# Row norm factors between two blocks: applied to the rows before the transpose, or where the products leave PSUM

## Chip, core and metric

One NeuronCore of one Trainium2 chip. The metric is the device time of one execution in microseconds (us), median of several runs. The engines are named as in the profile: PE (TensorE matmul), PEld (its weight load), DVE (VectorE), ACT (ScalarE), POOL (GpSimd), SP (SyncE, which here only issues DMAs).

## The reference

Two transformer-like blocks follow each other on 512 tokens of width 1024. The first ends with an RMS norm (gain `g_final`), the second begins with another (gain `norm_mix_g_2`) and a projection by `w_in_2`, whose output is cut into a GLU for a 31-tap causal convolution, queries, keys, values, forget logits and two gates:

```python
def rmsnorm(x, g):
    y = xf * lax.rsqrt(jnp.mean(xf * xf, axis=-1, keepdims=True) + EPS)
    return (y * g.astype(jnp.float32)).astype(x.dtype)

x = first_block(...)          # returns rmsnorm(x, g_final)
h = rmsnorm_2(x, norm_mix_g[l])
proj = h @ w_in[l]
u_glu, q, k, v, f_logit, gate_c, gate_a = jnp.split(proj, cuts, axis=-1)
```

A token's norm factor is one number for its row, so it commutes with the product by `w_in_2`. With s the mean square of x, and p that of x times `g_final`, the two norms together are x times `g_final` times `norm_mix_g_2` times one factor per token.

## The kernel before

All matrices are float32. In the second block a product is made of three: each operand is split into a rounded high part H and a low part L (`wsplit`, `split`), and `mm3` (line 86) issues H by H, H by L and L by H into one PSUM tile. A split is an ACT copy (line 131) and a subtraction (line 132) that POOL does, or DVE where said so.

`phase_b` is the first block's expert layer, eight pairs of experts. Its last pair ends with `last_down` (products line 1182, one PSUM tile for each half e of the width) and `scatter` (lines 1202 to 1216): the tile is scaled (y), split (yH on ACT, yL on DVE), multiplied by a 0/1 matrix P that puts rows back to their tokens, one product for each group t of 128 tokens, and added into `xres` by DVE (line 1216). Ahead of it, 16 small products and 4 ACT copies (lines 1234 and 1235) spread both gains over 128 partitions into `gg`.

`phase_c` begins with the norm. For each token group t and half e: `stage1` multiplies x by `g_final` (xg) and takes the sums of squares of x and xg on ACT (`sumsq`, line 1312); `stage2` makes the two factors r of the group (lines 1347 to 1351) and calls `put_T`, which multiplies xg by r and the second gain (hn, line 1323), transposes it on PE (line 1326) and splits it into `hx`, the moving operand of all projections. Then ACT writes xg times r back to `xres` (line 1363) and it goes to memory (`xrd`).

The projections follow: for each of 4 column tiles ct of the GLU a gate tile and a value tile (the first pair by `gemm_ws2`, in two halves of 256 tokens; the others by `ws_tile`, 24 products of 512 columns each), then the forget logits (fz), 8 tiles of queries and keys (`ev_qk`, line 1435), 4 of values by `gemm_ta`, and the gates. Their PSUM tiles come from a pool of four (tag "mm", `self.ps`); small products and transposes use another four (tag "at", `self.pa`). ACT empties every tile but the value tile of the GLU, which DVE multiplies by the gate (line 1381). Meanwhile DVE runs the convolution (lines 1400 to 1403): 31 taps for each ct, 124 instructions with 4 closing ones, in a row behind each other.

A scheduler sets the order of each engine's instructions at build time, with priorities (`tc.high_priority`) and hints (`tc.issue_after`); on the chip each engine takes its own instructions strictly in that order.

Of the kernel before, what the change touches and what calls it, by code (L numbers as in the profile page):

```python
# [8 lines left out]
F32 = mybir.dt.float32  # L9
# [8 lines left out]
EPS = 1e-6  # L18
# [27 lines left out]
XG = ((0, 0, 0, 0), (1, 1, 1, 1))  # L46
# [34 lines left out]
class Builder:  # L81
# [4 lines left out]
    def mm3(self, ps, l, r, first, last):  # L86
        mm = self.nc.tensor.matmul
        mm(ps, l[0], r[0], start=first, stop=False)  # L88
        mm(ps, l[0], r[1], start=False, stop=False)  # L89
        mm(ps, l[1], r[0], start=False, stop=last)  # L90
# [1039 lines left out]
    def phase_b(self, pb, right, G0):  # L1130
# [71 lines left out]
        def scatter(p, py):  # L1202

            P = xp.tile([128, 512], F32R, tag="PT", name="PT", bufs=1)
            V.tensor_scalar(P, self.iota, self.idxF[:, p:p + 1], None, op0=OP.is_equal)
            for e in range(2):
                y = xp.tile([128, 512], F32, tag="hid", name="y", bufs=3)
                V.scalar_tensor_tensor(y, py[e], self.valF[:, p:p + 1], ga2[:, e, :], op0=OP.mult, op1=OP.mult)  # L1208
                H, L = (xp.tile([128, 512], F32R, tag="yS", name=x, bufs=3) for x in ("yH", "yL"))
                AC.activation(out=H, in_=y, func=AF.Copy)  # L1210
                (nc.gpsimd if p < 7 else V).tensor_tensor(out=L, in0=y, in1=H, op=OP.subtract)  # L1211
                for t in range(4):
                    ps = self.pa()
                    self.mm2(ps, P[:, t * 128:(t + 1) * 128], (H, L), True, True)
                    c = slice(e * 512, (e + 1) * 512)
                    V.tensor_tensor((acc if p < 7 else xres)[:, t, c], (acc if p else xres)[:, t, c], ps, op=OP.add)
# [7 lines left out]
        for p in range(8):  # L1224
            hid = silu(pg)
            nxt = gather(p + 1) if p < 7 else None
            hT = hidden(hid, pair_mm(w_u, p, xT))
            if p == 7:
                gg = self.gg = self.rawp.tile([128, 2, 1024], F32, tag="raw", name="raw")
                for i in range(4):  # L1230
                    ps = self.pa()
                    for q in range(4):
                        r = 4 * i + q
                        nc.tensor.matmul(ps[:, q * 128:(q + 1) * 128], ident[0:16, r:r + 1].to_broadcast([16, 128]), rows2, start=True, stop=True)
                    AC.activation(out=gg[:, i // 2, (i % 2) * 512:(i % 2 + 1) * 512], in_=ps, func=AF.Copy)
# [40 lines left out]
    def phase_c(self, pc, right):  # L1276
# [34 lines left out]
        def sumsq(ss, src):  # L1311
            AC.activation(out=sm.tile([128, 512], F32, tag="nsq", name="nsq", bufs=2), in_=src, func=AF.Square, accum_out=ss)
# [18 lines left out]
        gf, g = self.gg[:, 0, :], self.gg[:, 1, :]  # L1331
        hx, ts = new_act()
        sss = [sm.tile([128, 2, 2], F32, tag="ss", name="ss", bufs=4) for _ in range(4)]
        xgs = [[tw(name="xg") for _ in range(2)] for _ in range(4)]
        r1s = {}

        def stage1(t, e):
            xs = xres[:, t, e * 512:(e + 1) * 512]
            (nc.gpsimd, V)[XG[e][t]].tensor_tensor(out=xgs[t][e], in0=xs, in1=gf[:, e * 512:(e + 1) * 512], op=OP.mult)
            sumsq(sss[t][:, 0, e:e + 1], xs)  # L1340
            sumsq(sss[t][:, 1, e:e + 1], xgs[t][e])

        def stage2(t):

            ss = sss[t]
            s, r = (sm.tile([128, 2], F32, tag=x, name=x, bufs=4) for x in ("s2", "r2"))
            V.tensor_tensor(s, ss[:, :, 0], ss[:, :, 1], op=OP.add)
            V.tensor_scalar(s, s, 1.0 / D, None, op0=OP.mult)
            V.tensor_scalar(s[:, 0:1], s[:, 0:1], EPS, None, op0=OP.add)
            V.scalar_tensor_tensor(s[:, 1:2], s[:, 0:1], EPS, s[:, 1:2], op0=OP.mult, op1=OP.add)  # L1350
            nc.gpsimd.tensor_tensor(out=r, in0=s, in1=self.mhalf.to_broadcast([128, 2]), op=OP.pow)
            r1s[t] = r[:, 0:1]
            put_T(ts, t, xgs[t], r[:, 1:2], g)
        for t in range(4):
            stage1(t, 0)
        stage1(0, 1)
        for t in range(4):
            if t < 3:
                stage1(t + 1, 1)
            stage2(t)  # L1360
        for t in range(4):
            for e in range(2):
                AC.activation(out=xres[:, t, e * 512:(e + 1) * 512], in_=xgs[t][e], func=AF.Copy, scale=r1s[t])

        xrd = self.drp.tile([512, 1024], F32, name="xrd")
        for t in range(4):
            nc.sync.dma_start(out=xrd[t * 128:(t + 1) * 128, :], in_=xres[:, t, :])
# [6 lines left out]
        def ev_gate(ct, ps):  # L1374
            glu[ct] = tw(name="glu")
            AC.activation(out=glu[ct], in_=ps, func=AF.Tanh, scale=0.5)

        def ev_a(ct, ps):
            u = sa.tile([128, 544], F32, tag="upad", name="upad", bufs=NST)
            nc.gpsimd.memset(u[:, 0:32], 0.0)  # L1380
            V.scalar_tensor_tensor(u[:, 32:544], glu[ct], 1.0, ps, op0=OP.add, op1=OP.mult)
            ups[ct] = u
        for c2 in (0, 256):
            rg, ra = self.cols_chunk(w, 512 + c2, 8, 256), self.cols_chunk(w, c2, 8, 256)
            for q in (0, 128):
                ct = (c2 + q) // 128
                pg, pa_ = (self.gemm_ws2([(rg, 0), (ra, 0)], hx) if ct == 0 else
                           (self.ws_tile(rg, q, hx, 8), self.ws_tile(ra, q, hx, 8)))
                ev_gate(ct, pg)
                ev_a(ct, pa_)  # L1390

# [26 lines left out]
        AC.activation(out=z, in_=ps[0:8], func=AF.Identity, bias=bf)  # L1418
# [21 lines left out]
        self.gemm_ta(w, 2048, hx, 8, 4, lambda t, ps: AC.activation(out=vt[t], in_=ps, func=AF.Copy))  # L1440
# [17 lines left out]
        on = sa.tile([128, 128], F32, tag="on128", name="on128", bufs=1)  # L1458
        V.memset(on, 1.0 / 512.0)
# [236 lines left out]
        V.memset(wrp, 0.0)  # L1696
        wr = wrp[:, :, 0:20]
        sel = sm.tile([128, 20], F32, tag="sel20", name="sel20", bufs=1)
        V.tensor_tensor(sel, ident[:, 0:20], ident[:, 32:52], op=OP.add)
        for q in (64, 96):  # L1700
            V.tensor_tensor(sel, sel, ident[:, q:q + 20], op=OP.add)
# [4 lines left out]
        V.tensor_tensor(wr, wr, gc.unsqueeze(2).to_broadcast([128, 8, 20]), op=OP.mult)  # L1706
# [461 lines left out]
```

## Time and profile before

| what | value |
|---|---|
| median of 3 runs | 1699.02 us (1697.12 to 1700.84) |
| the profiled execution, its own time | 1697.02 us |
| its span in the profile | 1695.0 us |
| granted TensorE clock, mean | 0.975 |
| PE busy | 92% of the span |
| DVE, ACT, POOL busy | 50%, 36%, 33% |

The span is read as a sequence of stages. Block boundary: from about 975 to 1031 us. The projections of the second block's input follow, with the convolution beside them, until about 1181 us, when the first attention scores come. In the timeline a row merges neighbours of one kind; PE records two rows for one float32 product and one for a product of H and L parts.

### The profile page before, as it was taken

The numbers are of one execution on the slowest core, as the hardware profiler recorded it, in microseconds if no ns is written. First come the engines' busy times: TensorE is split into PE (matmuls) and PEld (weight loads), VectorE is DVE, ScalarE is ACT, GpSimd is POOL, SyncE is SP. The second block draws the span as 40 slices with busy tenths as digits, with TensorE's granted clock in tenths as the row PEclk, the third lists the DMA queues.
The fourth block names the chain that finished last, engine by engine and source line by source line (L and its number), as shares of the span: only waits on it lengthen the run. The fifth ranks groups of instructions, "written<-read, shape, count | busy, mean of one in ns | idle before, by whom it ended". The sixth has DMA issues, their size and how long they took to land. (4 is left out here: it accounts for less than half of the span.)

```text
span 1695.0 us, 20847 instructions
## 1 busy us (share of the span) xinstructions
PE 1565.8 (92%) x7702; PEld 1043.6 (62%) x7702; DVE 854.0 (50%) x1567; ACT 615.4 (36%) x1281; POOL 565.9 (33%) x447
## 2 busy tenths in 40 slices
PE   6988899999999999999999979999999989789993
PEld 4766677777776344344434338777667766566662
DVE  4489654333562022202202148996755464667775
ACT  4433455433431000000000043325763354467773
POOL 1223233444431000000000024666342442657764
PEclk9989999999999999999999989999999999889997
DMA  9522314455666999999999974223111337379934
GB/s 318 166 97 94 128 62 135 152 164 181 242 233 255 397 409 408 409 409 409 409 409 409 390 237 144 81 75 100 50 59 54 124 132 278 127 257 347 345 135 166
DMA packets 165004, 381.23 MB, mean 225 GB/s; under 512 B 16270, under 2 KB 74710, under 8 KB 164892
## 3 DMA queue, kind: packets, MB, share of 16 engines
q1 hardware_dynamic: 160088, 371.50, 59.5%
q0 software_dynamic: 4320, 8.16, 1.3%
q8 instruction: 63, 1.03, 0.3%
q14 instruction: 49, 0.40, 0.1%
q10 hardware_dynamic: 484, 0.13, 0.0%
HBM read 367.40 MB, written 19.93 MB: 229 GB/s over the span
## 5 line engine op out<-in xcount | busy, mean ns | idle before, releaser
L132 POOL TENSOR_TENSOR wL<-raw,wH 128x512 fp32r<-128x512 f32 x220 | 312.7, 1427 | 410.3 <-ACT wH L131 392.0
L131 ACT ACTIVATE wH<-raw 128x512 fp32r<-128x512 f32 x240 | 149.3, 628 | 257.6 <-PE ps L89 142.7
L1154 PE MATMUL ps<-raw,xT 128*64 128x512 f32 x1024 | 240.8, 595 | 0.0
L1154 PEld LDWEIGHTS ps<-raw,xT 128*64 128x64 f32 x1024 | 74.3, 137 | 137.2 <-issue 133.5
L1211 POOL TENSOR_TENSOR yL<-y,yH 128x512 fp32r<-128x512 f32 x14 | 17.9, 1280 | 419.3 <-ACT yH L1210 409.1
L90 PE MATMUL ps<-raw,wL 128*128 128x512 f32 (+1 forms) x320 | 120.8, 377 | 3.0 <-POOL wL L132 3.0
L1208 DVE SCALAR_TENSOR_TENSOR y<-ps,valF,ga 128x512 f32<-128x512 f32 x16 | 12.0, 750 | 220.9 <-PE ps L1154 206.8
L88 PE MATMUL ps<-raw,wH 128*128 128x512 f32 (+1 forms) x320 | 121.8, 380 | 0.7 <-ACT raw L190 0.7
L89 PE MATMUL ps<-raw,wH 128*128 128x512 f32 (+1 forms) x320 | 121.2, 379 | 0.0
L1402 DVE SCALAR_TENSOR_TENSOR cacc<-upad,dwc,cacc 128x512 f32<-128x512 f32 x120 | 117.5, 1032 | 0.9
L1154 PE MATMUL ps<-raw,hidT 128*64 128x512 f32 x448 | 109.2, 594 | 2.8 <-DMA raw<-in_w_down_e 2.8
L90 PE MATMUL ps<-hx,wL 128*128 128x512 f32 x224 | 89.4, 399 | 2.3 <-POOL wL L132 2.3
L88 PE MATMUL ps<-hx,wH 128*128 128x512 f32 x224 | 90.7, 405 | 0.6 <-ACT wH L131 0.6
L1988 POOL TENSOR_TENSOR dL<-raw,dH 128x512 fp32r<-128x512 f32 x64 | 81.6, 1294 | 27.8 <-ACT dH L1987 27.3
L1968 DVE TENSOR_TENSOR wL<-raw,wH 128x512 fp32r<-128x512 f32 x96 | 88.3, 974 | 4.8 <-ACT wH L1967 3.5
L89 PE MATMUL ps<-hx,wH 128*128 128x512 f32 x224 | 89.4, 399 | 0.0
L1210 ACT ACTIVATE yH<-y 128x512 fp32r<-128x512 f32 x16 | 10.0, 627 | 207.1 <-DVE y L1208 207.1
L1193 ACT ACTIVATE hidT<-pa 128x512 f32<-128x512 f32 x16 | 9.6, 597 | 204.9 <-PE pa L1192 204.9
L1154 PEld LDWEIGHTS ps<-raw,hidT 128*64 128x64 f32 x448 | 36.2, 137 | 73.4 <-issue 62.7
L90 PEld LDWEIGHTS ps<-raw,wL 128*128 128x128 f32 x320 | 61.2, 191 | 15.0 <-POOL wL L132 3.4
L88 PEld LDWEIGHTS ps<-raw,wH 128*128 128x128 f32 x320 | 61.6, 192 | 12.2 <-ACT raw L190 1.1
L89 PEld LDWEIGHTS ps<-raw,wH 128*128 128x128 f32 x320 | 61.5, 192 | 11.4 <-issue 0.5
(615 smaller groups left out, 3397.4 us busy)
## 6 DMA issues: line engine op xcount, KB each, us to landing
raw<-in_w_gate_e SPq DMA_DIRECT2D x64, 1024.0 KB
raw<-in_w_up_e SPq DMA_DIRECT2D x64, 1024.0 KB
raw<-in_w_down_e SPq DMA_DIRECT2D x64, 1024.0 KB
raw<-in_w_in SPq DMA_DIRECT2D x34, 1024.0 KB
raw<-in_w_ada SPq DMA_DIRECT2D x24, 1024.0 KB
raw<-in_expert_w_gate SPq DMA_DIRECT2D x32, 512.0 KB
raw<-in_expert_w_up SPq DMA_DIRECT2D x32, 512.0 KB
raw<-in_expert_w_down SPq DMA_DIRECT2D x16, 1024.0 KB
```

The costliest lines, as they stand in the source:

```text
L88: mm(ps, l[0], r[0], start=first, stop=False)
L89: mm(ps, l[0], r[1], start=False, stop=False)
L90: mm(ps, l[1], r[0], start=False, stop=last)
L131: i = self.nc.scalar.activation(out=H, in_=raw_ap, func=AF.Copy)
L132: j = (eng or self.lsub).tensor_tensor(out=L, in0=raw_ap, in1=H, op=OP.subtract)
L1154: nc.tensor.matmul(ps[o, :], act[:, k, o], r[:, q, h * 512:(h + 1) * 512], start=k == 0, stop=k == 7, tile_position=(0, 64 * i))
L1208: V.scalar_tensor_tensor(y, py[e], self.valF[:, p:p + 1], ga2[:, e, :], op0=OP.mult, op1=OP.mult)
L1210: AC.activation(out=H, in_=y, func=AF.Copy)
L1211: (nc.gpsimd if p < 7 else V).tensor_tensor(out=L, in0=y, in1=H, op=OP.subtract)
L1402: V.scalar_tensor_tensor(acc, src, c, acc, op0=OP.mult, op1=OP.add)
L1968: V.tensor_tensor(out=L3, in0=w, in1=H3, op=OP.subtract)
L1988: (nc.gpsimd, V)[DL[i]].tensor_tensor(out=L, in0=src, in1=H, op=OP.subtract)
```

## The change

The rows are transposed as they are, times the product of the two gains (now a column factor on the transposed tile, `gs2`), without the token factors. The second norm's factor of all 512 tokens is spread over the partitions as `rbc` by one product of a diagonal matrix (`dg`), after the first pair of tiles. Each projection that has tokens along the columns is multiplied by it where it leaves PSUM (`times_r`, on DVE, high priority); the values take it as ACT's scale. The transposes of the first half go ahead of the second half's scatter, the first pair of tiles is done by `glu_first` in 512 columns, ACT's writes of `xres` go behind the first two gates, and some small DVE work for the router goes behind a mark.

```diff
@@ scatter
+                with self.tc.issue_after(self.x0T[1]) if (p, e) == (7, 1) else ExitStack():
+                    for t in range(4):
...
+                if (p, e) == (7, 0):
+                    pss = []
+                    for k in range(4):
+                        ps = (self.ps, self.pa)[k // 2]()
+                        for t in range(4):
+                            i = nc.tensor.transpose(ps[:, t * 128:(t + 1) * 128], xres[:, t, k * 128:(k + 1) * 128], ident)
+                        pss.append(ps)
+                    self.x0T = pss, i.ins
@@ last pair
-                for i in range(4):
+                for i in range(2):
...
+                ps = self.pa(16)
+                nc.tensor.transpose(ps, rows2, ident[0:16, 0:16])
+                gc = xp.tile([128, 16], F32, tag="gc2", name="gc2", bufs=1)
+                AC.activation(out=gc, in_=ps, func=AF.Copy)
+                V.tensor_tensor(self.gs2, gc[:, 0:8], gc[:, 8:16], op=OP.mult)
@@ start of phase_c
+        def put_x(e):
...
+                H = ts[0][e][:, q, :]
+                i = AC.activation(out=H, in_=ps, func=AF.Copy, scale=self.gs2[:, k:k + 1])
+                V.scalar_tensor_tensor(ts[1][e][:, q, :], ps, self.gs2[:, k:k + 1], H, op0=OP.mult, op1=OP.subtract)
+            return i.ins
+        with tc.issue_after(put_x(0)):
+            for t in range(2):
+                squares(t, 0)
+        with tc.issue_after(put_x(1)):
+            for t, e in ((2, 0), (3, 0), (0, 1), (1, 1), (2, 1), (3, 1)):
+                squares(t, e)
...
+        def times_r(out, ps, n=128):
+            with tc.high_priority(offset=400):
+                V.tensor_tensor(out, ps, rbc[0:n], op=OP.mult)
@@ projections
-            glu[ct] = tw(name="glu")
-            AC.activation(out=glu[ct], in_=ps, func=AF.Tanh, scale=0.5)
+            g = glu[ct] = tw(name="glu")
+            times_r(g, ps)
+            th = AC.activation(out=g, in_=g, func=AF.Tanh, scale=0.5)
+            V.scalar_tensor_tensor(g, g, 1.0, rbc, op0=OP.add, op1=OP.mult)
...
-            V.scalar_tensor_tensor(u[:, 32:544], glu[ct], 1.0, ps, op0=OP.add, op1=OP.mult)
+            self.mark = V.tensor_tensor(u[:, 32:544], glu[ct], ps, op=OP.mult).ins
...
+        def glu_first(rs):
+            pss = [self.ps() for _ in rs]
+            for kk in (0, 4):
+                for j, r in enumerate(rs):
+                    H, L = self.wsplit(r[:, kk:kk + 4, 0:128], 4, 128, (nc.gpsimd, V)[E2[2 * j + kk // 4]])
...
+            with tc.issue_after(i.ins):
+                ps = self.pa()
+                nc.tensor.matmul(ps, on, dg, start=True, stop=True)
+            AC.activation(out=rbc, in_=ps, func=AF.Copy, scale=512.0)
...
-        AC.activation(out=z, in_=ps[0:8], func=AF.Identity, bias=bf)
+        times_r(z, ps[0:8], 8)
+        AC.activation(out=z, in_=z, func=AF.Identity, bias=bf)
...
-            AC.activation(out=qk[ct], in_=ps, func=AF.Copy)
+            times_r(qk[ct], ps)
...
-                    AC.activation(out=new(ct), in_=self.ws_tile(r, q, hx, 8), func=AF.Tanh, scale=0.5)
+                    o = new(ct)
+                    times_r(o, self.ws_tile(r, q, hx, 8))
+                    AC.activation(out=o, in_=o, func=AF.Tanh, scale=0.5)
```

How the change moves instructions, at three places. Line numbers in these rows are those of the kernel that the row comes from.

PE at the end of the first block, before (hidT: last products of the experts; yH, yL by PT: the scatter; ident by hn: the transposes):

```order
L1182 MATMUL ps<-raw,hidT 64x512 x17
L95 MATMUL pa<-yH,PT 128x512 x4
L1182 MATMUL ps<-raw,hidT 64x512 x7
L96 MATMUL pa<-yL,PT 128x512 x2
L1182 MATMUL ps<-raw,hidT 64x512
L96 MATMUL pa<-yL,PT 128x512 x2
L1182 MATMUL ps<-raw,hidT 64x512 x7
L95 MATMUL pa<-yH,PT 128x512 x4
L96 MATMUL pa<-yL,PT 128x512 x4
L1326 MATMUL pa<-ident,hn 128x128 x12
L88 MATMUL ps<-raw,wH 128x256
```

and with the change (ident by xres: the transposes):

```order
L1181 MATMUL ps<-raw,hidT 64x512 x25
L94 MATMUL pa<-yH,PT 128x512
L95 MATMUL pa<-yL,PT 128x512
...
L1223 MATMUL ps<-ident,xres 128x128
L1181 MATMUL ps<-raw,hidT 64x512 x7
L1223 MATMUL ps<-ident,xres 128x128 x7
L1223 MATMUL pa<-ident,xres 128x128 x8
L94 MATMUL pa<-yH,PT 128x512 x2
L95 MATMUL pa<-yL,PT 128x512 x2
...
L1363 MATMUL pa<-ident,xres 128x128 x8
L87 MATMUL ps<-raw,wH 128x512
```

The scatter of the first half now stands in one piece, and the 16 transposes of that half stand ahead of the second half's scatter.

ACT after those transposes, with the change (nsq: squares; raw from pa: emptied transposes; wH: high parts of the weights for the first pair of tiles):

```order
L1327 ACTIVATE nsq,sst<-xg 128x512
L130 ACTIVATE wH<-raw 128x512
L1365 ACTIVATE raw<-pa,gs_840 128x512 x4
L1327 ACTIVATE nsq,sst<-xres 128x512
L1327 ACTIVATE nsq,sst<-xg 128x512
...
L1327 ACTIVATE nsq,sst<-xres 128x512
L1327 ACTIVATE nsq,sst<-xg 128x512
L130 ACTIVATE wH<-raw 128x512 x4
```

Of the four weight splits of the first pair one stands ahead of the last twelve squares, three behind them.

DVE beside the query and key tiles, with the change (cacc: the convolution; qk from ps: a tile leaves PSUM; fc from fe: forget sums):

```order
L1459 SCALAR_TENSOR_TENSOR cacc<-upad,dwc,cacc 128x512 x16
L1460 TENSOR_SCALAR cacc<-cacc,cols_721 128x512
L1459 SCALAR_TENSOR_TENSOR cacc<-upad,dwc,cacc 128x512
L1457 TENSOR_SCALAR cacc<-upad,dwc 128x512
L1396 TENSOR_TENSOR qk_7338<-ps,rbc 128x512
L1485 CAST fc<-fe 8x512 x2
L1486 TENSOR_TENSOR fc<-fe,fc 8x512 x2
L1396 TENSOR_TENSOR qk_7373<-ps,rbc 128x512
L1396 TENSOR_TENSOR qk_7410<-ps,rbc 128x512
L1396 TENSOR_TENSOR qk_7445<-ps,rbc 128x512
L1459 SCALAR_TENSOR_TENSOR cacc<-upad,dwc,cacc 128x512 x3
L1396 TENSOR_TENSOR qk_7482<-ps,rbc 128x512
```

Before, no tile of queries or keys passed through DVE. Now the first of them leaves PSUM behind 69 taps of the convolution, the fifth behind 72, the last behind 94, and the first gate behind all 120.

## Rows read from the trace of the kernel before

**Rows 1.** The page: busy time of each engine.

```profile
PE 1565.8 (92%) x7702; PEld 1043.6 (62%) x7702; DVE 854.0 (50%) x1567; ACT 615.4 (36%) x1281; POOL 565.9 (33%) x447
```

**Rows 2.** Busy time by stretch, from the block boundary to the first scores.

```profile
core 0: us, PE busy (x) PEld busy (x) DVE busy (x) ACT busy (x) POOL busy (x), PEclk, DMA share, GB/s
998.00:1004.00 6.00, 2.27 (x9) 1.42 (x8) 4.76 (x10) 5.71 (x19) 0.80 (x5) 1.00 0.16 22
1004.00:1014.00 10.00, 3.48 (x14) 2.68 (x15) 8.90 (x23) 8.67 (x21) 2.81 (x4) 0.53 0.35 72
1014.00:1018.00 4.00, 4.00 (x20) 3.90 (x20) 2.41 (x9) 3.14 (x8) 2.74 (x3) 0.50 0.33 131
1018.00:1031.00 13.00, 11.96 (x99) 11.61 (x99) 5.96 (x11) 6.63 (x13) 4.42 (x5) 0.99 0.48 163
1031.00:1093.00 62.00, 62.00 (x269) 47.89 (x268) 61.37 (x65) 21.27 (x34) 33.96 (x23) 1.00 0.33 102
1093.00:1140.00 47.00, 44.04 (x183) 35.13 (x182) 46.87 (x50) 11.97 (x21) 34.61 (x16) 0.96 0.30 90
```

**Rows 3.** Timeline of PE at the boundary: start, length, engine, line, operation, wait.

```profile
994.49 3.65 PE L1182 MATMUL ps<-raw,hidT 128*64 128x512 f32 x14
999.64 1.21 PE L95 MATMUL pa<-yH,PT 128*128 128x512 f32 x4 [1.51 <-ACT yH L1210]
1007.83 1.97 PE L1326 MATMUL pa<-ident,hn 128*128 128x128 f32 x8 [6.05 <-DVE hn L1323]
1013.60 0.58 PE L88 MATMUL ps<-raw,wH 128*128 128x256 f32 x1 [0.69 <-ACT raw L190]
...
1030.74 0.28 PE L90 MATMUL ps<-raw,wL 128*128 128x256 f32 x1
1030.86 0.39 PE L88 MATMUL ps<-raw,wH 128*128 128x512 f32 x1
1031.09 0.39 PE L89 MATMUL ps<-raw,wH 128*128 128x512 f32 x1
```

**Rows 4.** DMA rate (last column) in two single microseconds at the boundary.

```profile
988.00:989.00 1.00, 1.00 (x5) 0.38 (x5) 0.11 (x1) 0.00 (x0) 0.00 (x0) 1.00 1.03 383
990.00:991.00 1.00, 1.00 (x8) 0.35 (x5) 0.00 (x0) 0.00 (x0) 0.00 (x0) 1.00 1.08 347
```

**Rows 5.** Line 1312, the squares: nanoseconds min/median/max.

```profile
L1312 ACT ACTIVATE nsq<-xg x8: 612/616/625, 998.0 to 1015.6; 128x512 f32<-128x512 f32 x8
```

**Rows 6.** Timeline of DVE from the scatter's last sums to the scores.

```profile
1001.13 2.48 DVE L1216 TENSOR_TENSOR xres<-acc,pa 128x512 f32<-128x512 f32 x4 [0.81 <-PE pa L96]
...
1031.13 0.69 DVE L1381 SCALAR_TENSOR_TENSOR upad<-glu,ps 128x512 f32<-128x512 f32 x1 [6.23 <-PE ps L90]
...
1098.39 8.02 DVE L1402 SCALAR_TENSOR_TENSOR cacc<-upad,dwc,cacc 128x512 f32<-128x512 f32 x12
...
1181.25 0.59 DVE L1525 TENSOR_TENSOR s<-s,mask_n 128x128 f32<-128x128 f32 x2 [12.06 <-PE s L1524]
```

**Rows 7.** DVE's groups by form, 1031 to 1169: busy, mean ns, idle before.

```profile
L1402 DVE SCALAR_TENSOR_TENSOR cacc<-upad,dwc,cacc 128x512 f32<-128x512 f32 x120 | 117.5, 1032 | 0.9
L1403 DVE TENSOR_SCALAR cacc<-cacc,cols 128x512 f32<-128x512 f32 x4 | 4.0, 999 | 0.0
L1428 DVE TENSOR_TENSOR fc<-fe,fc 8x512 fp32r<-8x512 f32 x2 | 3.3, 1660 | 0.1
L1427 DVE CAST fc<-fe 8x512 fp32r<-8x512 f32 x2 | 2.9, 1436 | 0.0
```

**Rows 8.** Lines 1402 and 1381, each instruction: nanoseconds min/median/max.

```profile
L1402 DVE SCALAR_TENSOR_TENSOR cacc<-upad,dwc,cacc x120: 714/741/1868, 1033.4 to 1166.9; 128x512 f32<-128x512 f32 x120
...
L1381 DVE SCALAR_TENSOR_TENSOR upad<-glu,ps x4: 671/676/687, 1031.1 to 1076.8; 128x512 f32<-128x512 f32 x4
```

**Rows 9.** ACT's timeline: the first gate and the fourth query or key tile leave PSUM.

```profile
1028.63 0.58 ACT L1376 ACTIVATE glu<-ps 128x512 f32<-128x512 f32 x1
...
1092.75 0.58 ACT L1435 ACTIVATE qk<-ps 128x512 f32<-128x512 f32 x1
```

**Rows 10.** Timeline of POOL, one merged row.

```profile
1098.50 17.40 POOL L132 TENSOR_TENSOR wL<-raw,wH 128x512 fp32r<-128x512 f32 x5 [0.31 <-ACT wH L131]
```

**Rows 11.** What PE waited for, 1031 to 1169: total us, times, longest.

```profile
PE ps L90 <- POOL wL L132: 3.0, 1, 3.0
```

More of the change, by code (lines that the diff above doesn't have):

```diff
@@ L89, in mm3 @@
         mm(ps, l[0], r[1], start=False, stop=False)
-        mm(ps, l[1], r[0], start=False, stop=last)
+        return mm(ps, l[1], r[0], start=False, stop=last)
     def mm2(self, ps, one, r, first, last):
@@ L1311, in sumsq @@
         def sumsq(ss, src):
-            AC.activation(out=sm.tile([128, 512], F32, tag="nsq", name="nsq", bufs=2), in_=src, func=AF.Square, accum_out=ss)
+            AC.activation(out=tw(name="nsq"), in_=src, func=AF.Square, accum_out=ss)
         def new_act():
@@ L1328, in put_T @@
                 self.split(ps.rearrange("p (k s) -> p k s", k=4), (ts[0][e][:, :, tk], ts[1][e][:, :, tk]))
[L1331 removed]
+        gf = self.gg[:, 0, :]
         hx, ts = new_act()
[L1333 removed]
+        sst = sm.tile([128, 4, 2, 2], F32, tag="sst", name="sst", bufs=1)
         xgs = [[tw(name="xg") for _ in range(2)] for _ in range(4)]
[L1335 to L1341 removed]
@@ L1343, in stage2 @@
[L1343 to L1347, printed above, removed]
-            V.tensor_scalar(s, s, 1.0 / D, None, op0=OP.mult)
[L1349 to L1361, printed above, removed]
+        on = sa.tile([128, 128], F32, tag="on128", name="on128", bufs=1)
+        V.memset(on, 1.0 / 512.0)
+        def put_x(e):
+            for q in range(4):
+                k = 4 * e + q
+                if e == 0:
+                    ps = self.x0T[0][q]
+                else:
+                    ps = self.pa()
+                    for t in range(4):
+                        nc.tensor.transpose(ps[:, t * 128:(t + 1) * 128], xres[:, t, k * 128:(k + 1) * 128], ident)
+                H = ts[0][e][:, q, :]
+                i = AC.activation(out=H, in_=ps, func=AF.Copy, scale=self.gs2[:, k:k + 1])
+                V.scalar_tensor_tensor(ts[1][e][:, q, :], ps, self.gs2[:, k:k + 1], H, op0=OP.mult, op1=OP.subtract)
+            return i.ins
@@ new lines, in phase_c @@
+        s, r12 = (sm.tile([128, 4, 2], F32, tag=x, name=x, bufs=1) for x in ("s2", "r12"))
+        rbc = sa.tile([128, 512], F32, tag="rbc", name="rbc", bufs=1)
+        with tc.high_priority(offset=400):
+            V.tensor_tensor(s, sst[:, :, :, 0], sst[:, :, :, 1], op=OP.add)
+            V.tensor_scalar(s, s, 1.0 / D, None, op0=OP.mult)
+            V.tensor_scalar(s[:, :, 0], s[:, :, 0], EPS, None, op0=OP.add)
+            V.scalar_tensor_tensor(s[:, :, 1], s[:, :, 0], EPS, s[:, :, 1], op0=OP.mult, op1=OP.add)
+            sf, rf = (x.rearrange("p t a -> p (t a)") for x in (s, r12))
+            nc.gpsimd.tensor_tensor(out=rf, in0=sf, in1=self.mhalf.to_broadcast([128, 8]), op=OP.pow)
+            dg = tw(name="dg")
+            for t in range(4):
+                V.tensor_scalar(dg[:, t * 128:(t + 1) * 128], ident, r12[:, t, 1:2], None, op0=OP.mult)
@@ L1362, in phase_c, with residual @@
+        def times_r(out, ps, n=128):
+            with tc.high_priority(offset=400):
+                V.tensor_tensor(out, ps, rbc[0:n], op=OP.mult)
+        xrd = self.drp.tile([512, 1024], F32, name="xrd")
+        def residual(t):
             for e in range(2):
-                AC.activation(out=xres[:, t, e * 512:(e + 1) * 512], in_=xgs[t][e], func=AF.Copy, scale=r1s[t])
-        xrd = self.drp.tile([512, 1024], F32, name="xrd")
-        for t in range(4):
+                AC.activation(out=xres[:, t, e * 512:(e + 1) * 512], in_=xgs[t][e], func=AF.Copy, scale=r12[:, t, 0:1])
```

45 lines of the change are left out of this document (28 added, 17 removed).

## Prediction

> **What bounds the kernel now.** I read the page's busy shares first: PE works 92% of the span [rows 1], so a change pays only where PE waits, or runs at the low clock. The table by stretch shows such a place: from 998 to 1018 PE is busy 9.75 of 20 us, and its granted clock falls to 0.53 and 0.50, the 1.2 GHz level [rows 2]. The timeline tells what ends the waits. The last expert product ends at 998.1 (994.49 + 3.65), PE stands idle for 6.05 us until a normed row is there, and full width work begins only at 1030.86 [rows 3]. That is 32.7 us for 96 half-width products which at the pace of its last rows (0.12 us each, from 1030.74 to 1030.86) need 11.5. So up to 21 us lie open there, and the change aims at them.
>
> Behind the boundary the picture is another one. From 1031 to 1093 PE and DVE are both busy throughout (62.00 and 61.37 of 62 us), to 1140 DVE still 46.87 of 47 [rows 2]. DVE has no slack there; it gets 12.06 us at the very end, where it waits for the first scores [rows 6]. In this stretch PE waits once, 3.0 us [rows 11], since ACT, not DVE, empties its tiles. The convolution sets DVE's pace: 120 taps at a mean of 1032 ns [rows 7], though one alone takes 714 to 741 [rows 8]. A tap is stretched, to 1868 ns at most, when POOL makes a low part of the weights.
>
> **Part 1, the boundary.** Eight small products and two copies less save nothing, because the next products wait for weights: the DMA rate steps from 383 to 347 GB/s between 988 and 991 [rows 4], where the transfers change from one kind of matrix to the next, so the last expert weights land near 989. Counted from there: the scatter of half 0 in one piece (8 products of 0.23, two switches, 2.2 us), then 7 expert products at 0.45 (3.65 for 14 records, [rows 3]), end at 994.3 instead of 998.1. From there to the last sum into `xres` it took 5.5 us (998.1 to 1001.13 + 2.48, [rows 3, 6]); one more ACT and one more DVE instruction stand in front of the scatter's own, so I take 6.1: 1000.4. Then ACT empties four tiles (0.58 each, [rows 9], and 0.8 for PSUM buffers that must come free): 1003.6; makes twelve squares, 0.61 each [rows 5], 7.3 us: 1010.9; and the second weight split: 1011.5. PE has used up the first split by then. Of 48 products of 512 columns 36 are left, 0.23 us each (1030.86 to 1031.09, [rows 3]), 8.3 us, with 0.8 for POOL's low part and 1.3 for a start at the low clock: the first pair is done at 1021.9, not 1030.9. **Gain 9.0.** Bounds: 36 products all at half clock leave a gain of 1.5; squares that do not hold PE up would make it 14.
>
> Added on PE: one product that spreads `rbc`, 0.9 (four passes of 0.23).
>
> **Part 2, DVE.** All the rest of the change is hidden only if DVE keeps up, and here PE's PSUM tiles go to an engine that is full. What DVE gets before the convolution ends: 13 products by `rbc` (4 gates, 1 logits, 8 queries and keys), 4 second products on the gates, 4 small router steps. Before, DVE's first step on a tile began at 1031.13, 0.27 after the pair's end. Now four steps precede it (product 1.2, ACT copy 0.6, DVE 0.68, tanh 0.58, DVE 0.7): a **lag of 3.5**.
>
> A product by `rbc` reads one operand from PSUM. The nearest row is the value tile's, which took 671 to 687 ns every time, in the same stretch in which the taps were stretched [rows 8]; I take 0.68. A gate's second product reads SBUF twice, as a tap does: 1.03.
> The Trainium skill (SBUF — State Buffer, "Who interferes with whom") says that a DVE instruction with at most one SBUF input does not contend with GpSimd, and one with two does, the loser being blocked for the whole instruction. The two rows agree; without that rule the 13 products would cost 1.03 too, 4.6 us more in all.
>
> Now the place that decides. PSUM has four tiles for these products. The fifth tile of queries and keys can start only when the first has left, and that stands on DVE behind 69 taps. Before, 70 taps were done at 1106.4 (1098.39 + 8.02, with 13, 1, 14, 16, 2, 1, 9, 1 and 1 ahead of these 12) [rows 6]. For the change: one tap less (-1.0), a closing and an opening step of the convolution more (+2.0, [rows 7]), four products (+2.7), three second products (+3.1), the tile's own (+0.7), the lag (+3.5): 1117.4 on the clock of before. PE would start that fifth tile when the fourth is complete, at 1092.7 [rows 9], with the 0.9 at 1093.6. It would wait 23.8 us. But while PE stands still, POOL gets no weights to split and a tap takes 0.74 or less instead of 1.03; I take a quarter off. **First wait 17.5**, part of it already at the third tile, whose weight split stands on ACT behind the logits' first step.
>
> After that DVE has four forget steps (3 to 6 us, [rows 7]), three products (2.0), 25 taps (25.8 at 1.03) and four products (2.7) until the eighth tile is out, 35 us; PE makes four tiles of 24 products (22.3) and nine products of the values (2.1) until it needs that tile. With a relief as above I take a **second wait of 6** (3 to 10). The gates then find DVE free: behind 94 taps 26 are left, some 30 us, and four tiles of PSUM cover them.
>
> Part 3, the rest: eight tanh on tiles for the attention get a DVE step more in a stretch where PE is the bound; the router's loads and steps move to where nothing waits; the writes of `xres` and its four DMAs go 10 us later, ahead of weights that are needed 40 us after. Zero, up to 3 if DVE holds up scores.
>
> **Sum.** -9.0 + 0.9 + 17.5 + 6 = +15.4. The profiled execution took 1697.0 (span 1695.0 and 2.0 around it), so 1712.4; the median of the runs is 2.0 above that execution, which gives 1714.
>
> **Rivals.**
> 1. *DVE keeps up* (18%). If POOL and DVE got in each other's way less than in this trace, taps would run at 0.70 to 0.74 and 69 of them would be done in time; the first wait shrinks to about 2, the second to none: -9 + 1 + 2 = -6, 1693. For it: between 1098 and 1106 12 taps took 8.02 us, 0.67 each [rows 6]. Against it: POOL's five low parts then took 17.40 us [rows 10], and PE waited 3.0 for them [rows 11]. The point at which it decides is DVE's mean for a tap: below about 0.8 us there is no wait worth a name.
> 2. *The waits nearly cancel the gain* (8%): waits of 8 to 10 in all, for example because DVE catches up faster in the first: 1697 to 1701.
> 3. *The clock falls in the new waits* (8%). At the boundary, 6 us without work were followed by 0.53 and 0.50 until 1018 [rows 2]: at half pace 4 us of products cost 2 more. Two such waits cost 4: 1718. The Trainium skill (TensorE: Matmul & The Clock Gate, the summary "Why this matters for your kernels") asks for no idle gaps between bursts of products, since they bring the throttled state back; by that rule both waits would pay it, and rows 2 agree for the one gap there.
> 4. *The boundary gains little* (6%): the squares and the half clock take it, gain 2 instead of 9: 1721.
>
> **How the numbers follow.** The forecast has 60%, its own range 1704 to 1722 (waits of 15 to 28, gain of 5 to 12). A measurement of this kernel can tell about 0.2%, 3.4 us, from no change. Faster by more: rival 1, and a little of rival 2: 0.19. Within: most of rival 2: 0.07. Slower: the rest, 0.74. The range from 1697 to 1725 takes in the forecast, rivals 3 and 4 and most of rival 2, and leaves out rival 1.
>
> **What would show it.** In the profile of the changed kernel: the first pair ends 5 to 12 us earlier; PE waits 10 to 20 us at the start of the fifth query and key tile with a DVE release (line 1396), and some more in the first products of the values; DVE is busy without a gap from the first pair to the end of the convolution; POOL has a gap where PE waits. It is wrong if PE runs without a wait from the first pair to the scores.

## The result, and the profile after

The changed kernel took 1710.9 us (median of 4 runs, 1707.9 to 1712.2) against 1698.4: a ratio of 1.0071, 95% interval 1.0057 to 1.0085. It is slower by 12.5 us; forecast were 1714 and +15.4. The profiled execution took 1710.27, its span is 1708.3 and so 13.3 longer than before. The page's busy times have hardly moved against [rows 1]:

```profile
PE 1563.0 (91%) x7641; PEld 1042.6 (61%) x7641; DVE 857.5 (50%) x1581; ACT 611.6 (36%) x1273; POOL 577.7 (34%) x448
```

The table by stretch does show it. It has the columns and the stretches of [rows 2]:

```profile
998.00:1004.00 6.00, 5.08 (x25) 3.10 (x25) 5.77 (x11) 6.00 (x15) 1.57 (x7) 1.00 0.62 133
1004.00:1014.00 10.00, 5.13 (x16) 3.92 (x15) 6.61 (x9) 10.00 (x30) 7.07 (x6) 0.66 0.23 70
1014.00:1018.00 4.00, 3.99 (x18) 2.98 (x17) 2.46 (x4) 1.34 (x4) 3.85 (x4) 1.00 0.27 93
1018.00:1031.00 13.00, 13.00 (x57) 10.40 (x56) 10.10 (x13) 7.78 (x13) 7.67 (x6) 1.00 0.70 238
1031.00:1093.00 62.00, 53.44 (x220) 40.35 (x218) 61.04 (x75) 17.60 (x28) 33.31 (x15) 0.92 0.21 69
1093.00:1140.00 47.00, 34.09 (x129) 27.03 (x130) 42.14 (x55) 6.32 (x10) 25.79 (x15) 0.82 0.30 90
```

Up to 1031 PE does more than before and sees less of the low clock. From 1031 to 1140 it is busy for 87.5 us where it was for 106.0, and the granted clock falls to 0.92 and 0.82 on the mean. DVE is full to 1093, as before; behind that it has a gap, to which the text comes back.

**The boundary.** PE's timeline, from the last expert product to the end of the first gate/value pair:

```profile
992.63 3.65 PE L1181 MATMUL ps<-raw,hidT 128*64 128x512 f32 x14
...
1001.71 1.36 PE L1363 MATMUL pa<-ident,xres 128*128 128x128 f32 x8 [0.19 <-DVE xres L1216]
...
1009.28 0.79 PE L89 MATMUL ps<-raw,wL 128*128 128x512 f32 x1 [4.87 <-DVE wL L131]
1009.87 0.63 PE L87 MATMUL ps<-raw,wH 128*128 128x512 f32 x1
...
1022.03 1.02 PE L1433 MATMUL pa<-dg,on 128*128 128x512 f32 x2
```

The pair is complete at 1022.0, before at 1030.86 [rows 3]: 8.8 us gained. The one wait of note, 4.9 us, is for the first low part, which DVE makes:

```profile
1006.15 3.08 DVE L131 TENSOR_TENSOR wL<-raw,wH 128x512 fp32r<-128x512 f32 x1
```

It takes 3.08 us there and 0.68 eight us later; POOL was making its products of rows and norm weights at the time.

**Behind it.** What PE waited for from 1031 to 1170 (us in total, times, longest), which before was 3.0 us in all [rows 11]:

```profile
PE ps L89 <- POOL wL L131: 9.7, 2, 8.7
PE ps L87 <- DVE qk L1396: 6.8, 2, 3.7
PE ps L87 <- ACT wH L130: 5.0, 1, 5.0
```

Those are 21.5 us under three names. The first scores start at 1194.8, before at 1180.9: of the way from the first pair to there, 172.8 us instead of 150.0, the boundary's gain is lost two and a half times over.

All three names lead to DVE's queue. The first wait is the third tile of queries and keys. Its weight split stands on ACT behind the logits' first step, and that waits for DVE's product, which is behind 42 taps. DVE's timeline, that product:

```profile
1072.54 0.67 DVE L1396 TENSOR_TENSOR fz<-ps,rbc 8x512 f32<-8x512 f32 x1
```

ACT's timeline, the logits' first step and the split behind it (two more steps of the logits and a table load lie between):

```profile
1073.24 0.72 ACT L1476 ACTIVATE fz<-fz,bf 8x512 f32<-8x512 f32 x1 [11.47 <-DVE fz L1396]
...
1076.48 0.61 ACT L130 ACTIVATE wH<-raw 128x512 fp32r<-128x512 f32 x1
```

And PE's timeline, the first products behind the two longest waits:

```profile
1077.14 0.79 PE L87 MATMUL ps<-raw,wH 128*128 128x512 f32 x1 [4.99 <-ACT wH L130]
...
1099.16 0.80 PE L89 MATMUL ps<-raw,wL 128*128 128x512 f32 x1 [8.66 <-POOL wL L131]
```

The second, 8.7 us in the middle of the fourth tile, is for a low part on POOL. One single step of POOL takes 14.56 us there (1.27 is the shortest of its kind), and it covers DVE's longest run of taps. POOL's timeline:

```profile
1084.55 14.56 POOL L131 TENSOR_TENSOR wL<-raw,wH 128x512 fp32r<-128x512 f32 x1
```

DVE's timeline at the same time:

```profile
1085.85 10.67 DVE L1459 SCALAR_TENSOR_TENSOR cacc<-upad,dwc,cacc 128x512 f32<-128x512 f32 x16
...
1097.91 0.67 DVE L1396 TENSOR_TENSOR qk<-ps,rbc 128x512 f32<-128x512 f32 x1
```

The run passes at 0.67 us a tap, undisturbed. POOL's step ends at 1099.11, half a us after the first DVE product that reads PSUM (1097.91 + 0.67). At that moment DVE also stops: its next step, a cast, waits for a tile that POOL clears only behind its splits. DVE's timeline:

```profile
1103.31 1.93 DVE L1485 CAST fc<-fe 8x512 fp32r<-8x512 f32 x2 [4.73 <-POOL fc L1474]
```

So these rows don't tell which of the two, the product or the stop, let POOL finish; and DVE, late already, lost 4.7 us more to POOL. The third wait, 3.0 and 3.7 us, is that of the values for the PSUM tiles of the last queries and keys. The DVE products that free these stand behind that gap, so a part of the 6.8 us is POOL's lateness handed on.

### The profile page after: what moved, and what is told of

It reads as the page before. It is cut to its first block, busy times and chain, and to the rows that moved or that the text cites. A ratio compares the mean times of both kernels' runs of the same rounds, so it can differ in the third digit from the quotient of the medians.

```text
span 1708.3 us, 20749 instructions
## 1 busy us (share of the span) xinstructions
PE 1563.0 (91%) x7641; PEld 1042.6 (61%) x7641; DVE 857.5 (50%) x1581; ACT 611.6 (36%) x1273; POOL 577.7 (34%) x448
## 5 line engine op out<-in xcount | busy, mean ns | idle before, releaser
L131 POOL TENSOR_TENSOR wL<-raw,wH 128x512 fp32r<-128x512 f32 x220 | 320.2, 1463 | 422.0 <-ACT wH L130 392.0
L87 PE MATMUL ps<-raw,wH 128*128 128x512 f32 (+1 forms) x304 | 118.8, 391 | 5.0 <-ACT wH L130 5.0
L88 PE MATMUL ps<-raw,wH 128*128 128x512 f32 (+1 forms) x304 | 118.5, 390 | 0.0
L1459 DVE SCALAR_TENSOR_TENSOR cacc<-upad,dwc,cacc 128x512 f32<-128x512 f32 x120 | 106.4, 936 | 0.4
L87 PEld LDWEIGHTS ps<-raw,wH 128*128 128x128 f32 x304 | 58.9, 194 | 16.4 <-ACT wH L130 5.4
L88 PEld LDWEIGHTS ps<-raw,wH 128*128 128x128 f32 x304 | 58.6, 193 | 11.4 <-issue 0.7
```

What stands on the lines that cost most here:

```text
L131: j = (eng or self.lsub).tensor_tensor(out=L, in0=raw_ap, in1=H, op=OP.subtract)
L1459: V.scalar_tensor_tensor(acc, src, c, acc, op0=OP.mult, op1=OP.add)
```

## Experiments

Times beside the runs are medians in us, each against runs of the kernel before on the same chip. Theory: the boundary gains about 9 us, and DVE's products, placed in a queue that is full, cost more.

**1. The boundary alone.** Factors left out, so that gates, logits, queries and keys leave PSUM by ACT:

```diff
-            times_r(qk[ct], ps)
+            AC.activation(out=qk[ct], in_=ps, func=AF.Copy)
```
(and the same for glu, fz, thc and tha; `upad` by one step as before)

> Leaves out the tokens' factor rbc on gates, logits, queries, keys and attention gates: those tiles leave PSUM through ACT in one step as in the kernel before; the new boundary stays. Theory (the boundary gains about 8 net, all the loss is DVE's products): 1690, 1687 to 1693; PE waits no more than 4 us between the first gate/value pair and the first scores, and the pair still ends near 1022. Rival (the boundary gives little, or its gain is lost in something else that moved, such as the writes of xres): 1697 or more.

Measured: 1684.7 against 1698.65, ratio 0.9920 (0.9904 to 0.9937). PE's waits for the weights' parts, 1015 to 1215:

```profile
PE ps L89 <- POOL wL L131: 4.4, 3, 3.2
PE ps L87 <- ACT wH L130: 0.9, 1, 0.9
```

With the factors left out the change gains 14 us, not 8: more than either theory gave. About 4 of the 6 between are faster products, which the boundary alone does not explain (last section).

**2. The products alone**, in the kernel before, with a tile of ones for `rbc`:

```diff
+        rbc = sa.tile([128, 512], F32, tag="rbc", name="rbc", bufs=1)
+        V.memset(rbc, 1.0)
-            AC.activation(out=qk[ct], in_=ps, func=AF.Copy)
+            times_r(qk[ct], ps)
```
(and the same for glu, fz, thc and tha; the squares' scratch has one buffer instead of two, for room)

> The kernel before, with the products by a tile of ones put where the change has its products (glu, logits, queries and keys, attention gates) and the gates' second product; the boundary is the old one and the result is the reference's. Theory (the products alone make PE wait some 20 us): 1712 to 1724, first pair at 1031 as before. Rival (the waits come from what else moved, the products alone are hidden): under 1702.

Measured: 1722.8 against 1698.65, ratio 1.0140 (1.0123 to 1.0157), 24 us. PE's waits have the same three names as in the changed kernel:

```profile
PE ps L90 <- POOL wL L132: 10.7, 2, 9.6
PE ps L88 <- DVE qk L1377: 6.6, 2, 4.3
PE ps L88 <- ACT wH L131: 5.4, 1, 5.4
```

So the loss needs nothing of the new boundary. Parts 1 and 2 of the prediction are shown apart: -14 (the faster products among it) and +24 make +10, where the change measured +12.5.

**3. Queries and keys by ACT**, in the changed kernel, their factor left out.

```diff
-            times_r(qk[ct], ps)
+            AC.activation(out=qk[ct], in_=ps, func=AF.Copy)
```

> The changed kernel with the eight queries and keys copied by ACT, so without their factor; logits, gates and the gates' second product stay on DVE. Theory (each product that stands behind taps holds up its own tile; the logits' and POOL's waits are other ones): the two waits on qk, 6.8 us, go, the 5.0 us behind the logits and the 8.7 us on POOL's low part stay: 1701 to 1706. Rival (DVE's whole load is the cause, 5.3 us less of it is all that counts): 1705 to 1708 with waits left on DVE. Rival (queries and keys are the only cause): 1692 or less.

Measured: 1701.75 against 1698.65. The waits on qk are gone, 11.0 us on POOL and 5.0 on ACT stay, as the first theory said.

**4. The logits by ACT**, in the changed kernel, their factor left out.

```diff
-        times_r(z, ps[0:8], 8)
-        AC.activation(out=z, in_=z, func=AF.Identity, bias=bf)
+        AC.activation(out=z, in_=ps[0:8], func=AF.Identity, bias=bf)
```

> The changed kernel with the logits straight from PSUM by ACT, so without their factor. Theory (ACT's weight split stood behind the logits' first step, which stood behind 36 taps on DVE): the waits of 5.0 and 1.1 us go and the half clock behind them (some 2 us): 1701 to 1706. Rival (the third query tile would only wait at the next place, for its PSUM tile or POOL): the first wait goes, another grows by as much, 1709 or more.

Measured: 1711.1 against 1697.64. The waits on ACT and POOL are both gone, and one name holds it all (PE's waits from here on, 1015 to 1290):

```profile
PE ps L87 <- DVE qk L1396: 25.4, 3, 20.4
```

The rival was right. The 20.4 us stand ahead of the fifth tile of queries and keys, the place that the prediction named.

**5. The runs of taps broken** by a small step that reads SBUF once.

```diff
+                    if ct in (1, 2) and i % 4 == 3:
+                        with tc.issue_after(t_.ins):
+                            V.tensor_reduce(out=sm.tile([128, 1], F32, tag="brk", name="brk", bufs=2), in_=rbc[:, 0:128], axis=mybir.AxisListType.X, op=OP.add)
```

> The changed kernel with the same small sums behind every fourth tap of the second and third channel tile and no other change of order. Theory (the 16 taps in one run hold one POOL step for 14.6 us, and that makes the wait of 8.7 us): that step falls under 5 us, the wait under 3, the others stay: 1701 to 1706. Rival (POOL is only slow because DVE is busy; each step more on DVE makes it later): the wait stays at 7 or more, 1711 to 1715.

Measured: 1714.6 against 1697.64. One half of the theory held: POOL's longest step is 4.79 us, and the wait of 8.7 is gone (the 1.1 left stood in the changed kernel too). The other did not: the time did not fall. PE's waits:

```profile
PE ps L87 <- DVE qk L1396: 17.5, 2, 12.3
PE ps L87 <- ACT wH L130: 3.6, 1, 3.6
PE ps L89 <- POOL wL L131: 1.1, 1, 1.1
```

What POOL no longer waited for, DVE did: a tap takes 0.994 us on the mean, 0.936 without the breaks, and PE waits for DVE instead. So the run of taps did hold POOL up, and yet with that gone PE's waits are 22.2 us in all, against 21.5. The run does not price the hold-up by itself: the 14 breaks put 3.8 us more on DVE, and its products on PE are slower (last section).

**6. The products earlier in DVE's order.** The taps are issued in pieces, each tied behind a product.

```diff
+        def taps_to(n, after=None):
+            with tc.issue_after(after) if after else ExitStack():
+                while done[0] < n:
+                    next(tg, None)
+                    done[0] += 1
...
-            times_r(qk[ct], ps)
+            i = times_r(qk[ct], ps)
+            nq[0] += 1
+            taps_to(AT[nq[0]], i)
```

> The changed kernel, result unchanged: the taps of the convolution are tied behind the products, so that the logits' product stands behind 28 taps (36 before), the first query tile's behind 36 (72), the last's behind 57 (98) and the attention gates' between the last 63 taps instead of behind all. Theory (the place in DVE's order makes the waits, not its load; the load has slack at the end): PE waits under 6 us from the first pair to the scores, 1689 to 1695. Rival (DVE's load is the bound): the waits move to the end of the convolution or to the gates, 1703 or more.

(The numbers in this table count a tile's opening step as a tap; the trace of the changed kernel has 42 taps ahead of the logits' product, not 36.) Measured: 1710.6 against 1698.65. In this kernel the convolution's norm is issued ahead of its last taps, so that part of the computation is another. PE's waits up to the scores fell to 2.9 us, and these start at 1169.8. But the table was one entry out, and the first attention gate's product stood behind 61 taps while PE made the values. DVE's timeline:

```profile
1134.73 0.69 DVE L1397 TENSOR_TENSOR thc<-ps,rbc 128x512 f32<-128x512 f32 x1 [21.62 <-PE ps L90]
```

DVE lost 21.6 us there, and the scores then waited for it (11.4 us at once). The run doesn't tell order from load.

**7. The same with the table put right.**

```diff
+AT = (28, 35, 37, 39, 41, 44, 47, 50, 52, 86, 92, 98, 104, 110, 116, 126, 126, 126)
```

> As f_order with another table: the last query or key product behind 52 taps, the first attention gate's behind 86 (61 in f_order, where DVE stood idle for 21.6 us while PE made the values), all taps ahead of the seventh gate's; the result is the reference's. Theory (only the place in DVE's order was wrong): PE waits under 4 us from the first pair to the scores, scores start at 1169 to 1173, the time is 1685 to 1691. Rival (DVE's load is the bound even so): waits at the first scores, 1697 or more. Rival (the 32 taps that now stand in one run while PE makes the values hold POOL's low parts off, as the 16 taps did in the changed kernel): a wait of 5 to 12 us on POOL among the values, 1692 to 1700.

Measured: 1702.3 against 1697.64, ratio 1.0030 (1.0020 to 1.0039). That is 4.7 us slower than before instead of 12.5, so the order is worth some 8 us of what the changed kernel had lost. PE runs from the first pair to the scores with 3.9 us of small waits, and then waits 9.1 (PE's waits, 1031 to 1200):

```profile
PE s L1597 <- ACT P L1604: 9.1, 1, 9.1
PE ps L90 <- POOL wL L132: 2.9, 5, 0.7
```

ACT waits there for the first scores' DVE steps, which stand behind the last taps. Those end at 1187, 14 us after PE's first score: with no wait left in between, DVE's load is the bound. The taps took 1.058 us on the mean, 1.032 before the change [rows 7]. The second rival (POOL held up among the values) fell: over runs of 18 and of 14 taps no step of POOL took more than 1.82 us.

**8. Order and breaks together** (the edits of 5 and 7).

> As g_order2, with a small sum over 128 columns of rbc on DVE behind every fourth tap from the 36th on, whose result nobody reads: a step that reads SBUF once, in a run of taps that read it twice. Theory (a run of taps without a break holds POOL's subtraction off to its end; a step between lets it in): no single POOL step over 5 us, no wait on POOL over 1.5 us, 1686 to 1692. Rival (steps between change nothing): as g_order2, and 2 to 5 us more if DVE is the bound.

Measured: 1707.6 against 1697.64. POOL's longest step is 2.91 us, but that was so in experiment 7 too, and the time rose by 5.3 us: the rival's outcome. Its reason, 22 steps more on a full DVE, is not shown: the products on PE are slower here too, which by the reckoning of the last section costs about 4 us.

**9. The running sum in PSUM.** Order as in 7; the taps now read SBUF once.

```diff
-                acc = xc[ct]
+                acc = self.pa(name="ca")
...
-                V.tensor_scalar(acc, acc, 0.5, self.dw_b[:, ct:ct + 1], op0=OP.mult, op1=OP.add)
+                V.tensor_scalar(xc[ct], acc, 0.5, self.dw_b[:, ct:ct + 1], op0=OP.mult, op1=OP.add)
```

> As g_order2, with the convolution's running sum in a PSUM tile (one each of four that stand empty here) instead of SBUF: a tap then reads SBUF once, as the products of queries and keys do, the result is the reference's. Theory (DVE and POOL hold each other up where both read SBUF twice over; the order and this are all that is wrong): a tap takes 0.66 to 0.76 us on the mean (1.06 in g_order2), POOL's steps 1.3, DVE waits for PE rather than PE for DVE, the wait of 9.1 at the second scores goes: 1685 to 1690. Rival (a running sum in PSUM costs DVE as much as POOL did): taps of 0.9 or more, 1698 or more.

Measured: 1685.1 against 1698.11, ratio 0.9926 (0.9910 to 0.9943), 17 us less than 7. The taps and POOL's low parts, each with nanoseconds min/median/max, of the changed kernel:

```profile
L1459 DVE SCALAR_TENSOR_TENSOR cacc<-upad,dwc,cacc x120: 714/739/1832, 1027.2 to 1160.9; 128x512 f32<-128x512 f32 x120
...
L131 POOL TENSOR_TENSOR wL<-raw,wH x50: 1268/1388/14557, 1028.1 to 1195.9; 128x512 fp32r<-128x512 f32 x50
```

and of this one:

```profile
L1462 DVE SCALAR_TENSOR_TENSOR ca<-upad,dwc,ca x120: 717/756/757, 1028.0 to 1166.9; 128x512 f32<-128x512 f32 x120
...
L132 POOL TENSOR_TENSOR wL<-raw,wH x55: 1272/1295/1862, 1028.7 to 1195.2; 128x512 fp32r<-128x512 f32 x55
```

No tap is stretched any more, and the longest of POOL's steps falls from 14.56 to 1.86. A sum in PSUM costs 0.04 us a tap where nobody disturbs (0.756 against 0.714), and saves 0.3 here (0.75 on the mean, 1.06 in experiment 7). No run has the sum in PSUM without the new order, so how much of this it would do alone is open.

**10. The running sum in PSUM in the kernel before**, as the control.

```diff
-            acc = tp(name="cacc")
+            acc = self.pa(name="ca")
```

> The kernel before with the convolution's running sum in PSUM and nothing else changed. Theory (before, PE waits on this pair of engines in one place only): taps of 0.66 to 0.76, the one wait of 3.0 us on POOL's low part goes with the clock behind it, DVE gets idle; 1693 to 1697. Rival (DVE's load costs before something too, for instance at the first scores): 1690 or less. Rival (no effect): 1697 to 1700.

Measured: 1694.5 against 1698.11, ratio 0.9978 (0.9969 to 0.9988). As the theory said: the wait of 3.0 us for POOL goes, and DVE gets 45 us of idle time at the scores, where it had 12 [rows 6]:

```profile
1177.68 0.59 DVE L1525 TENSOR_TENSOR s<-s,mask_n 128x128 f32<-128x128 f32 x2 [44.89 <-PE s L1524]
```

**11. A table for taps of that length.**

```diff
-AT = (28, 35, 37, 39, 41, 44, 47, 50, 52, 86, 92, 98, 104, 110, 116, 126, 126, 126)
+AT = (33, 41, 44, 48, 53, 59, 65, 71, 76, 106, 112, 118, 126, 126, 126, 126, 126, 126)
```

> As l_order_psum_acc with a table for taps of 0.7 us: the logits' product behind 33, the first query tile's behind 41, the last product of queries and keys behind 76, the first attention gate's behind 106, all taps ahead of the fourth gate's. Theory: no wait of PE over 1.5 us from the first pair to the scores, which start at 1167 to 1170; 1683 to 1688, the fastest of all with the whole computation. Rival (taps are slower than 0.76 and the queries wait again): 1690 or more.

Measured: 1684.7 against 1698.11, ratio 0.9924 (0.9907 to 0.9940). No better than 9 by more than the runs scatter; both beat the kernel before and the changed one, and with the sum in PSUM on both sides the change, new order included, is worth 9.8 us (1694.5 to 1684.7), about 4 of them by the faster products of the last section. PE waits twice from 1031 to 1170, 1.7 us for a query's product and 1.4 for a value's.

**12. The boundary once more**, on top of 11: the weight splits ahead of the squares, the first low part on POOL.

```diff
-E2 = (1, 1, 0, 0)
+E2 = (0, 1, 0, 0)
...
+                W1[j, kk] = self.wsplit(r[:, kk:kk + 4, 0:128], 4, 128, (nc.gpsimd, V)[E2[2 * j + kk // 4]])
+                wh = self.split_ins[0]
-        with tc.issue_after(put_x(1)):
+        with tc.issue_after(last), tc.issue_after(wh):
```

> As m_order2_psum_acc, with the boundary cut once more: all four weight splits of the first gate/value pair ahead of the twelve squares on ACT, and the first low part on POOL, ahead of its products of rows and norm weights, instead of on DVE. Theory (the first low part, 3.1 us on DVE beside POOL, and the twelve squares between the first split and the others hold PE up at the boundary by some 5 us together): PE's wait of 4.9 before the third product falls under 2, the first pair ends 3 to 5 us earlier, 1680 to 1682. Rival (the factors come later by as much, since the squares do, and the first products' tiles wait for them): the pair ends earlier, but PE waits as long for DVE three tiles on: 1683 to 1686.

Measured: 1687.7 against 1698.88, ratio 0.9939 (0.9925 to 0.9952): no gain over 11, and the theory's 1680 to 1682 is missed. The wait of 4.9 is gone, and a new one stands where the factors are spread over the partitions. PE's timeline:

```profile
1023.10 2.04 PE L1442 MATMUL pa<-dg,on 128*128 128x512 f32 x2 [4.46 <-DVE wfL L191]
```

The pair is complete at 1018.6 (1023.10 less 4.46), but `dg` comes from the squares and is ready at 1023.0 (1019.04 + 3.92 on DVE), and that product stands next in PE's order (the row names the DVE step that ran last, `wfL`). That is what the rival said would happen, but at another place: not three tiles on, but at once. The squares are on the path of the factors, so moving them only changes who waits.

## Why the prediction was right, and where its steps were off

The sign, the size (+15.4 against +12.5) and the range held. Point by point:

- *Part 1, gain 9.0*: the pair was forecast at 1021.9 and came at 1022.0. The way there was another one. Forecast were 36 products from 1011.5 on, behind the squares; in the trace the first low part held PE to 1009.28, 3.08 us long beside POOL, and the ten products behind that wait ran at half clock to 1013.6, so that the second split (ACT, 1012.4) was hardly missed. The last 36 products then began 2.1 us later than forecast, and took 8.5 us without the 2.1 that the forecast had added for a low part and a low clock: that the ends differ by only 0.1 is luck. Two causes end there at the same time, the low part and the split. Experiment 12 took both away.
- *The product that spreads `rbc`, 0.9*: 0.46 us until the next product starts, and 0.40 more until the one behind it does, as forecast.
- *Part 2, a product by `rbc` at 0.68*: 0.67 to 0.69 in every group; the gates' second product at 0.96, forecast 1.03.
- *The lag of 3.5*: the first value tile's step on DVE began at 1025.91, 3.9 after the pair instead of 0.27, so 3.6 later.
- *The first wait, 17.5, at the fifth tile*: here the name was wrong, and the time right by luck. The fifth tile was to start 17.5 after 1093.6 on the clock of before, less the 9.0 of the boundary: 1102.1. It started at 1102.9 (24 products a tile, counted from 1077.14). But the tile's own PSUM buffer was free at 1098.6, 3.5 us earlier than forecast; what held the tile up were 14.7 us of waits at three places ahead of it, with half clock behind them. The prediction had put only "part of it" at the third tile's weight split, and not seen that POOL could be the one that is late. Experiments 4 and 5 bring a wait back to the fifth tile, 20.4 and 12.3 us, while the waits by these names come to 25.4 and 22.2 in all, against 21.5: DVE's lateness reads as one quantity, and which instruction shows it depends on the order.
- *The second wait, 6 (3 to 10)*: 6.8, at the values, as forecast, though a part came by way of POOL and DVE's gap. Both waits together: 23.5 forecast, 21.5 measured, which is 18.5 more than the 3.0 of before.
- *Relief of a quarter*: the taps' mean fell from 1032 ns [rows 7] to 936, less than a quarter, while POOL had nothing to split or was itself held up. In experiment 7, where PE hardly stands still before the scores, it is 1058.
- *Rival 3, the clock*: this was not a rival but a part. Behind the waits the granted clock was 0.50, the 1.2 GHz level. Of the changed kernel, with the columns of [rows 2]:

```profile
1077.00:1085.00 8.00, 6.79 (x15) 4.91 (x16) 7.18 (x9) 4.19 (x7) 7.59 (x4) 0.50 0.00 0
1099.00:1102.00 3.00, 2.84 (x7) 2.26 (x8) 0.00 (x0) 0.00 (x0) 3.00 (x4) 0.50 0.54 118
1129.50:1139.50 10.00, 6.28 (x15) 4.40 (x15) 10.00 (x16) 0.63 (x1) 2.58 (x1) 0.50 0.18 63
```

  and of the kernel before, behind its one wait of 3.0:

```profile
1110.00:1114.00 4.00, 4.00 (x12) 3.09 (x12) 3.94 (x3) 0.59 (x2) 4.00 (x3) 0.57 0.10 8
```

  In the three stretches PE was busy for 15.9 us, so about 8 were lost; before, 1.7. The sum had left out these 6.3 us.
- *Rival 1, DVE keeps up*: its point of decision was a tap of 0.8 us. Experiments 9 and 11 make it so, 0.75, in another order of DVE, and give 1685, where the rival had 1693.
- *The signs*: the pair's end and the waits among the values came as named. PE did not wait at the fifth tile, and DVE was not busy without a gap: it stood idle for 4.73 us at 1098.6. POOL had nothing to do at PE's first wait, as named, but was itself what PE waited for at the second.

So the mechanism was right: the boundary gains, and waits for a DVE that is full take more than that. By what was measured the sum is -8.8 (boundary), +0.9 (the spread), +18.5 (waits), +6.3 (half clock) and -4.2 (faster products, last section), +12.7 where the medians differ by 12.5 and the first scores start 13.9 later. The step that was off is the one on the waits: 5 us too much in size, and two thirds of what was measured (14.7 of 21.5) at other instructions than named; the two terms left out, half clock and pace, come to +2.1. That the forecast missed by 3 us only is in part such cancelling.

On how DVE and POOL get in each other's way, the Trainium skill (SBUF — State Buffer, "Who interferes with whom") says that a DVE step with two SBUF inputs contends with a GpSimd step that reads SBUF, and that one with at most one does not, outside DVE's two-port modes; the prediction left that condition out. The closing steps of the convolution, which read one tensor, were stretched in the kernel before: 999 ns on the mean [rows 7], 470 the shortest; whether by such a mode no run shows. Experiment 9 agrees for the taps, on both sides: 757 ns at most instead of 1832 on DVE, 1.86 us at most instead of 14.56 on POOL. That page of the Trainium skill ("SBUF: two separate sides") lets the loser wait for one instruction; here a POOL step was held over a whole run, 14.56 us, and in experiment 7, over runs of 18 and 14 taps, none was. What decides that is not settled by these runs.

## What to carry to other kernels

Work moved off a path that waits is only free on an engine that has room in that very stretch: read its busy time there, and the steps that stand ahead of each moved step in its queue, not its share of the span (DVE: 50%). An in-order engine that is late shows under many names; before one of them is mended, ask whether the lateness goes or only moves, as in experiments 4, 5 and 12. And where a long chain on DVE runs beside POOL, a running sum in PSUM is worth a trial if banks stand empty: here it gave the change the room that it lacked, together with DVE's order put right: 26 us for the two (1710.9 to 1684.7).

## What the runs showed that was not expected

**Products run faster in most kernels with the new boundary.** Twelve products, from one low part on POOL to the next, take 2.80 us before and 2.72 in the changed kernel, both at a granted clock of 1.00. POOL's timeline of the kernel before:

```profile
1131.45 1.33 POOL L132 TENSOR_TENSOR wL<-raw,wH 128x512 fp32r<-128x512 f32 x1 [1.04 <-ACT wH L131]
1134.25 1.56 POOL L132 TENSOR_TENSOR wL<-raw,wH 128x512 fp32r<-128x512 f32 x1 [1.46 <-ACT wH L131]
```

and of the changed one:

```profile
1106.39 1.45 POOL L131 TENSOR_TENSOR wL<-raw,wH 128x512 fp32r<-128x512 f32 x1 [1.43 <-ACT wH L130]
1109.12 1.31 POOL L131 TENSOR_TENSOR wL<-raw,wH 128x512 fp32r<-128x512 f32 x1 [1.28 <-ACT wH L130]
1111.84 1.30 POOL L131 TENSOR_TENSOR wL<-raw,wH 128x512 fp32r<-128x512 f32 x1 [1.41 <-ACT wH L130]
```

The kernels with the old boundary (experiments 2 and 10) have 2.80 too, and most with the new one, such as experiments 1, 7 and 9, have 2.72. But experiments 5 and 8 have the new boundary, and 2.80. POOL's timeline of experiment 5, where the granted clock is 1.00 as well:

```profile
1113.12 1.29 POOL L131 TENSOR_TENSOR wL<-raw,wH 128x512 fp32r<-128x512 f32 x1 [1.09 <-ACT wH L130]
1115.92 1.71 POOL L131 TENSOR_TENSOR wL<-raw,wH 128x512 fp32r<-128x512 f32 x1 [1.51 <-ACT wH L130]
1118.72 1.29 POOL L131 TENSOR_TENSOR wL<-raw,wH 128x512 fp32r<-128x512 f32 x1 [1.09 <-ACT wH L130]
```

These two differ from the changed kernel and from experiment 7 only by the breaks on DVE and the small tile that these write. So the new boundary, with its rows that are not normed, does not by itself make the products fast, and the cause stays open. Over some 620 products between the first pair and the scores the difference is 4 us (620 by 0.0067): most of the surplus of experiment 1, and a part of what experiments 5 and 8 seem to cost.

**POOL can be starved by DVE for longer than a step**: 14.56 us over 16 taps, 1.27 alone. The kernel before has such a step too, of 11.16 us. The other way round a tap took 1.83 us at most.
